# A two-layer hybrid encoder on one core: gate rows by block and head, and the first layer's row sums from a token-major copy of x

## The chip, the core and the metric

One Trainium2 chip, one of its cores. The metric is the device time of one execution of the program in microseconds, as the median of several runs.

## The reference, cut to what matters

512 tokens of width 1024 go through two layers. A layer normalises the rows of x, projects them to 6,928 columns, gives those to four mixers (A a gated linear recurrence, B windowed attention, C an mLSTM, D attention to 256 memory tokens), multiplies each by a SiLU gate, projects their concatenation back and adds x. The change touches two pieces.

```python
def _rmsnorm(x, g):
    xf = x.astype(F32)
    y = xf * lax.rsqrt(jnp.mean(xf * xf, axis=-1, keepdims=True) + EPS)
    return (y * g.astype(F32)).astype(x.dtype)
...
        b = jnp.cumsum(fb, axis=-1)
        d_intra = jnp.where(mask, b[..., :, None] - b[..., None, :] + ib[..., None, :], -jnp.inf)
        d_inter = b + m[..., None]
        m_t = jnp.maximum(jnp.max(d_intra, axis=-1), d_inter)
        w = jnp.einsum('bhtd,bhsd->bhts', qb, kb) * jnp.exp(d_intra - m_t[..., None])
        g = jnp.exp(d_inter - m_t)
```

The first is the row norm of layer 0. The second is C's gates: for 4 heads and 2 directions, running sums `b` of the log forget gates over 512 tokens and a running maximum `m_t` that stabilises the exponentials.

## The kernel before, in words

Everything works on float32 split into two float32r halves, hi and lo. A projection is three matmuls per 128-row step (hi by hi, hi by lo, lo by hi); `proj_ch` (L435) makes channel-major results 128x512, `proj_tok` (L399) token-major ones 128x256. `load_w` (L374) brings a weight block of 512 KB into a tile `wr` (3 buffers), ScalarE casts it to `wh`, VectorE subtracts to `wl` (3 buffers each).

The order of the work is made by a planner, `Weave` (L153): the main line emits projections and calls `tick` with their TensorE nanoseconds; jobs are generators that yield (TensorE time spent, latency until their next step), and a job's next step is emitted when the planned time has passed. The constants `G_LAT*`, `R_LAT*`, `M_LAT*` are those latencies. Each engine then runs its own queue in that order.

**The opening** (`start`, L1401). For each of 8 steps k: x^T's rows (`xs`, 128x512) and a weight step of 256 columns are loaded on SP's queue; ScalarE makes hi, VectorE lo of both; TensorE multiplies the *unnormalised* rows for the first A projection (six matmuls a step, tiles `o`). Beside it the squares of x^T go alternately to ScalarE and GpSimd, GpSimd and VectorE add them (`plus`, L1422), and `add_squares` (L470) sums over channels with four ones products (tile `tr`, 128x1). `rms4` and `diag` make 1/rms as a diagonal matrix and `spread` (L493) broadcasts it with one ones product to R, 128x512. All that is the job "R" (`rest`, L1458); after the spread it also forms the normalised rows `h` (`norm_k`, L504: a product with R on VectorE or, for odd k, GpSimd; hi on ScalarE; lo on VectorE), then the squares and the spread of the memory rows (Rm). Meanwhile the main line (`group_A`, L674; `gates`, L697) projects the two gate directions from the unnormalised rows and scales the results by R. The first projection on normalised rows is `values` (L713).

**C's gate chain** (`gate_chain`, L925), a job in each layer, woven among the window attention of B (`mix_B`, L788) and projections. Its rows are 4 heads at partitions 0 to 3 (forward) and 32 to 35 (backward), 512 tokens each: a polynomial for log(1+y), four transposes per 128 tokens (L950), four scans of 4x512 on VectorE, differences and exponentials, eight transposes back (L1013). The rows R and G go through HBM (`rdr`, `gdr`) to be broadcast later, the block decays through `ddr` to `dec`.

## Time and profile before

| | us |
|---|---|
| median of 3 runs | 1123.88 (1120.58 to 1124.38) |
| the profiled execution | 1126.58 |
| its span, first to last instruction | 1124.7 |
| TensorE busy | 1083.0 (96%) |
| VectorE busy | 780.0 (69%) |
| ScalarE busy | 538.7 (48%) |
| GpSimd busy | 140.8 (13%) |

The profile is of one execution. PE is TensorE's matmuls, PEld its weight loads, DVE VectorE, ACT ScalarE, POOL GpSimd, SP the queue that issues transfers. Matmuls are pipelined: one shows the time from start to end, and the next starts earlier. A bracket at the end of a timeline row is the idle time before it on its engine and what ended it. L142 is the line of a helper that records every operation of four engines, so rows are read by their tiles: `u` and `a` are work tiles, `pj`, `tr`, `s` and `o` the four kinds of PSUM tiles.

### The profile page before, as it was taken

Reading aid. Unit: us, or ns where it says so; the run is one execution under the profiler, and the core shown is the slowest. Engines: PE = TensorE matmul, PEld = TensorE weight load, DVE = VectorE, ACT = ScalarE, POOL = GpSimd, SP = SyncE. Lnnn points to the kernel's source line nnn. Section 1 sums busy time; section 2 is a strip of 40 time slices with the busy share of each in tenths; the row PEclk is TensorE's granted clock in tenths of the full one; section 3 lists DMA queues with packets and bytes.
Section 4 is the critical chain, followed back from the end, with each engine's and each line's share of the span. In section 5 each row is a group of like instructions: output and inputs, shape, how many; then the busy total and the mean of one; then the engine's idle time right before and its main releaser. Section 6 shows DMA issues by size and latency. Waiting matters only on the chain.

```text
span 1124.7 us, 22824 instructions
## 1 busy us (share of the span) xinstructions
PE 1083.0 (96%) x9142; PEld 972.2 (86%) x9142; DVE 780.0 (69%) x1815; ACT 538.7 (48%) x1138; POOL 140.8 (13%) x212
## 2 busy tenths in 40 slices
PE   6899999989999999999999999999899999999997
PEld 4699988989888797888788999889889788989997
DVE  7788546787476968777373676477858678687664
ACT  5544346656444444334554433376655353433443
POOL 4200000231000213011020000012200012120200
PEclk9899999999999999999999999999999999999999
DMA  7232134111221435222434221221122233362111
GB/s 260 76 114 77 57 112 133 59 58 58 94 66 56 120 105 170 92 90 87 138 129 134 76 79 56 94 78 57 40 75 78 76 90 108 94 197 86 66 38 75
DMA packets 34785, 105.44 MB, mean 94 GB/s; under 512 B 4360, under 2 KB 7816, under 8 KB 34680
## 3 DMA queue, kind: packets, MB, share of 16 engines
q1 hardware_dynamic: 33960, 101.57, 28.6%
q0 software_dynamic: 720, 2.42, 0.5%
q8 instruction: 72, 1.18, 0.4%
q14 instruction: 33, 0.27, 0.1%
HBM read 99.72 MB, written 4.26 MB: 92 GB/s over the span
## 4 chain that ended last, share of the span: by engine, by line
PE 77%; DVE 13%; ACT 3%; issue 2%; DMA 1%; POOL 0%; SPq 0%; DVEq 0%; ACTq 0%; POOLq 0%
PE pj L248 32%; PE pj L251 29%; DVE a L142 5%; PE o L248 4%; PE s L248 3%; PE s L251 3%; DVE u L142 3%; DVE wl L142 3%; PE tr L858 1%; PE o L251 1%; ACT a L142 1%; ACT wh L142 1%; ACT u L142 1%; DVE rq_t L142 1%; PE tr L1291 1%
## 5 line engine op out<-in xcount | busy, mean ns | idle before, releaser
L251 PE MATMUL pj<-wh,u 128*128 128x256 f32 x1984 | 389.2, 287 | 1.8 <-ACT u L142 1.2
L248 PE MATMUL pj<-u,wh 128*128 128x512 f32 (+1 forms) x1216 | 378.4, 392 | 1.2 <-ACT a L142 1.0
L251 PEld LDWEIGHTS pj<-wh,u 128*128 128x128 f32 x1984 | 316.7, 189 | 6.0 <-ACT u L142 1.6
L142 DVE TENSOR_TENSOR wl<-wr,wh 128x1024 fp32r<-128x1024 f32 (+1 forms) x162 | 197.0, 1217 | 132.0 <-ACT wh L142 130.9
L251 PE MATMUL pj<-wl,u 128*128 128x256 f32 x992 | 280.7, 283 | 0.0
L248 PEld LDWEIGHTS pj<-u,wh 128*128 128x128 f32 x1216 | 219.7, 191 | 43.0 <-ACT a L142 1.4
L142 ACT CAST wh<-wr 128x1024 fp32r<-128x1024 f32 (+1 forms) x162 | 164.2, 1014 | 154.4 <-PE pj L248 85.0
L248 PE MATMUL pj<-u,wl 128*128 128x512 f32 (+1 forms) x608 | 234.3, 385 | 1.8 <-DVE wl L142 1.8
L251 PEld LDWEIGHTS pj<-wl,u 128*128 128x128 f32 x992 | 188.3, 190 | 0.8 <-issue 0.3
L248 PEld LDWEIGHTS pj<-u,wl 128*128 128x128 f32 x608 | 115.4, 190 | 25.2 <-DVE wl L142 2.0
L142 DVE TENSOR_TENSOR u<-u,a 128x512 f32<-128x512 f32 (+1 forms) x104 | 74.1, 730 | 19.7 <-PE s L251 15.9
L142 POOL TENSOR_SCALAR u<-u,rB 128x256 f32<-128x256 f32 (+1 forms) x64 | 37.4, 597 | 240.6 <-DVE rB L142 137.2
L248 PE MATMUL pj<-wh,u 128*128 128x256 f32 (+1 forms) x320 | 62.8, 287 | 0.0
L248 PE MATMUL o<-u,u 128*128 128x129 f32 (+1 forms) x384 | 51.9, 281 | 2.1 <-DVE dnC L142 2.1
L248 PEld LDWEIGHTS o<-u,u 128*128 128x128 f32 x384 | 49.7, 196 | 4.7 <-issue 2.7
L142 POOL TENSOR_TENSOR u<-u,cf 128x512 f32<-128x512 f32 x16 | 24.2, 1510 | 234.1 <-DMA u<-rdr 234.1
L248 PEld LDWEIGHTS pj<-wh,u 128*128 128x128 f32 x320 | 51.0, 188 | 0.7 <-issue 0.5
L248 PE MATMUL pj<-wl,u 128*128 128x256 f32 (+1 forms) x160 | 45.3, 284 | 0.0
L142 DVE TENSOR_TENSOR u<-u,u 128x512 f32<-128x512 f32 (+2 forms) x48 | 38.8, 841 | 3.8 <-ACT a L142 2.6
L248 PE MATMUL s<-u,a 128*128 128x256 f32 (+1 forms) x224 | 41.3, 303 | 0.0
L251 PEld LDWEIGHTS s<-u,u 128*32 128x32 f32 (+1 forms) x1760 | 27.4, 115 | 14.9 <-issue 6.0
L142 DVE TENSOR_TENSOR u<-pj,u 128x256 f32<-128x256 f32 (+2 forms) x52 | 24.9, 502 | 21.4 <-PE pj L248 14.6
(212 smaller groups left out, 1440.2 us busy)
## 6 DMA issues: line engine op xcount, KB each, us to landing
wr<-in_wpk SPq DMA_DIRECT2D x154, 512.0 KB, 3.5
u<-in_xT SPq DMA_DIRECT2D x16, 256.0 KB, 4.5
u<-rdr SPq DMA_DIRECT2D x16, 256.0 KB, 4.6
u<-gdr SPq DMA_DIRECT2D x16, 192.0 KB, 4.5
u<-in_memT SPq DMA_DIRECT2D x4, 512.0 KB
xd<-u POOLq DMA_DIRECT2D x4, 512.0 KB, 5.2
u<-xd SPq DMA_DIRECT2D x4, 512.0 KB, 9.2
out<-u SPq DMA_DIRECT2D x8, 256.0 KB, 2.0
```

Of the source, the lines that this page charges most:

```text
L142: r = f(*args, **kw)
L248: nc.tensor.matmul(out, l, r, start=start, stop=stop)
L251: nc.tensor.matmul(out, l, r, start=start, stop=stop, skip_group_check=True)
L858: nc.tensor.transpose(pt[:, j * P:(j + 1) * P], pr[e][:, j * P:(j + 1) * P], ident)
L1291: nc.tensor.transpose(pt[:, (2 * t + i) * P:(2 * t + i + 1) * P], pr[:, i, t * P:(t + 1) * P], ident)
```

## The change

It has two parts.

C's gate chain keeps a row per block of 128 tokens and head: 16 rows at partitions 0 to 15 (forward), 16 at 32 to 47 (backward), each 128 tokens long. One transpose takes the place of four, the scans run over 128 tokens in 16 rows, and the carry from block to block is made by two matmuls of 48x49 (with constant matrices that say which block comes earlier), a masked add and a maximum. Two transposes bring the rows back. These tiles use the PSUM kind `o` in place of `tr`. G's exponential takes the carried maximum as its bias. The decays go to HBM and come back in 4-byte pieces, in another layout.

In the opening, x itself is loaded too, token-major, four tiles of 128x1024 (`xt`); ScalarE squares each with an accumulating output, which gives the row sums. The squares of x^T, their additions and the four ones products go. The normalised rows are a job of their own, "N", eight steps with 1.1 us planned between them, all products on VectorE; `gates` joins it before the mixers start. The squares of the memory rows follow the spread of R, and their spread becomes the first step of the job `mem_norm`.

```diff
-G_LAT0, G_LAT1, G_LAT2, G_LAT3, G_LAT4 = 2800, 1800, 2250, 2250, 3400
+G_LAT0, G_LAT1, G_LAT2, G_LAT3, G_LAT4 = 2800, 6500, 2500, 4500, 4500
...
-R_LAT0, R_LAT = 6000, 3500
-M_LAT, M_LAT2 = 20000, 2500
+R_LAT0, R_LAT = 0, 9000
+H_LAT = 1100
+M_LAT, M_LAT2 = 20000, 1500
...
             if pr == 0:
                 gates()
+                wv.join(*jobN)
+                jobN.clear()
...
-                for c in range(NC):
-                    nc.tensor.transpose(pt[0:100, c * P:(c + 1) * P], GP[:, c], ident)
-                act.copy(LI[0:36], pt[0:36])
-                act.copy(L[0:36], pt[64:100])
-                yield 0, G_LAT2
+                pt = po()
+                nc.tensor.transpose(pt[0:112, 0:P], GP, ident)
+                act.copy(LI[0:48], pt[0:48, 0:P])
+                act.copy(L[0:48], pt[64:112, 0:P])
+                yield 107, G_LAT2
...
-                dve.tensor_tensor_scan(M[0:4], L[0:4], LI[0:4], 0.0, ALU.add, ALU.max)
-                dve.tensor_tensor_scan(rev(M), rev(L), rev(LI), 0.0, ALU.add, ALU.max)
-                dve.tensor_tensor_scan(B[0:4], KM[0:4], L[0:4], 0.0, ALU.mult, ALU.add)
-                dve.tensor_tensor_scan(rev(B), rev(KM), rev(L), 0.0, ALU.mult, ALU.add)
+                dve.tensor_tensor_scan(B[0:16], one, L[0:16], 0.0, ALU.mult, ALU.add)
+                dve.tensor_tensor_scan(rev(B), ones[32:48], rev(L), 0.0, ALU.mult, ALU.add)
+                dve.tensor_tensor_scan(M[0:16], L[0:16], LI[0:16], NEG, ALU.add, ALU.max)
+                dve.tensor_tensor_scan(rev(M), rev(L), rev(LI), NEG, ALU.add, ALU.max)
+                ends = [(slice(32 * d, 32 * d + 16), (P - 1) * (1 - d)) for d in range(2)]
+                for r, e in ends:
+                    dve.tensor_scalar(X2[r, 0:49], succ[r], B[r, e:e + 1], None, ALU.mult)
+                    dve.tensor_scalar(X2[r, 49:98], ident[r, 0:49], M[r, e:e + 1], None, ALU.mult)
                 yield 0, G_LAT3
...
-                dve.tensor_tensor(R[0:36], B[0:36], M[0:36], ALU.subtract)
+                pS = po()[0:48, 0:49]
+                mm(pS, pred, X2[0:48, 0:49], start=True, stop=False)
+                mm(pS, ones[0:48, 0:48], X2[0:48, 49:98], start=False, stop=True)
...
+                dve.tensor_tensor(ca[0:48], pS, gmask, ALU.add)
+                dve.tensor_reduce(mb[0:48], ca[0:48], AX.X, ALU.max)
+                dve.scalar_tensor_tensor(M[0:48], B[0:48], mb[0:48], M[0:48], ALU.add, ALU.max)
...
+                dve.tensor_tensor(R[0:48], B[0:48], M[0:48], ALU.subtract)
...
-                for tt, n in ((TA, 100), (TB, 36)):
-                    pt = ptr()
-                    for c in range(NC):
-                        nc.tensor.transpose(pt[:, c * n:c * n + n], tt[0:n, c * P:(c + 1) * P], ident[0:n, 0:n])
...
+                yield 250, G_LAT4
+                pt = po()
+                nc.tensor.transpose(pt[:, 0:112], TA[0:112], ident[0:112, 0:112])
+                nc.tensor.transpose(pt[:, 112:160], TB[0:48], ident[0:48, 0:48])
...
         def mem_norm():
             yield 0, 0
+            spread(jobM.pop(0), Rm)
+            yield 450, M_LAT2
             mem0.append(mem_kv(0))
...
-                sqs.append(a2([512]))
-                if k % 2 == 1:
-                    act.activation(sqs[k], x, AF.Square)
-                    if k < 6:
-                        plus(gp, k - 1, k)
-                else:
-                    gp.tensor_tensor(sqs[k], x, x, ALU.mult)
-                if k == 5:
-                    plus(dve, 0, 2)
-                elif k == 7:
-                    for j in (4, 6, 7):
-                        plus(dve, 0, j)
...
+            xt, mt = [[u4([D]) for _ in range(n)] for n in (NC, 2)]
...
+            def squares(ts, ss):
+                for c, t in enumerate(ts):
+                    act.activation(t, t, AF.Square, accum_out=ss[:, c:c + 1])
...
             def rest():
 
+                squares(xt, sst)
                 with tc.high_priority():
-                    add_squares(sums, sqs[0], NC, True, True)
-                    dg = diag(rms4(sums[:, 0:NC]), NC)
-                yield 900, R_LAT
+                    dg = diag(rms4(sst), NC)
+                yield 0, R_LAT
                 with tc.high_priority():
                     spread(dg, R)
                     for b in range(2):
                         dve.tensor_tensor(q[b], pts[b], R, ALU.mult)
+                squares(mt, ssm)
+                jobM.append(diag(rms4(ssm, 2), 2))
+                jobN.append(wv.spawn("N", norms()))
+                yield 900, 0
+
+            def norms():
                 for k in range(8):
-                    norm_k(xs[k // 2][:, k % 2], k, R, 0, h, gp if k % 2 else dve)
+                    norm_k(xs[k // 2][:, k % 2], k, R, 0, h, dve)
+                    yield 0, H_LAT
```

The order moves in three places. First SP's queue in the opening; `wr_265`, `wr_271` (before) and `wr_250`, `wr_256` (after) are the weights of the first gate projection, `wr_403`, `wr_409` and `wr_361`, `wr_367` those of the second. Before:

```order
L142 DMA wr_265<-in_wpk 128x1024
L142 DMA wr_271<-in_wpk 128x1024
L142 DMA u_40_245<-in_mem 128x1024
L142 DMA u_41_246<-in_mem 128x1024
L142 DMA u_44_251<-in_cu 128x288
L142 DMA wr_403<-in_wpk 128x1024
L142 DMA wr_409<-in_wpk 128x1024
L142 DMA wr_473<-in_wpk 128x1024
```

After:

```order
L152 DMA wr_250<-in_wpk 128x1024
L152 DMA wr_256<-in_wpk 128x1024
L152 DMA u_30_220<-in_x 128x1024
L152 DMA u_31_221<-in_x 128x1024
L152 DMA u_32_222<-in_x 128x1024
L152 DMA u_33_223<-in_x 128x1024
L152 DMA u_34_224<-in_mem 128x1024
L152 DMA u_35_225<-in_mem 128x1024
L152 DMA u_40_236<-in_cu 128x288
L152 DMA wr_361<-in_wpk 128x1024
L152 DMA wr_367<-in_wpk 128x1024
L152 DMA wr_455<-in_wpk 128x1024
```

The four rows of x stand between the first projection's weights and everything that follows, and the second projection's weights are seven places behind.

Second, TensorE in the opening, inside the first gate projection (tiles `s_277`, `s_278` before, `s_262`, `s_263` after), which starts right after the 48 matmuls of the weight loop. Before, from behind its second matmul on:

```order
L251 MATMUL tr_137<-ones,a_31_145 128x1 x4
L248 MATMUL s_277<-u_5_98,wl_267 128x512
L248 MATMUL s_277<-u_5_98,wh_266 128x512
L248 MATMUL s_277<-u_9_102,wh_266 128x512
L248 MATMUL s_277<-u_5_98,wl_267 128x512
L248 MATMUL s_277<-u_6_99,wh_266 128x512
L248 MATMUL s_277<-u_10_103,wh_266 128x512
L248 MATMUL s_277<-u_6_99,wl_267 128x512
L248 MATMUL s_277<-u_6_99,wh_266 128x512
L248 MATMUL s_277<-u_10_103,wh_266 128x512
L248 MATMUL tr_330<-a_60_322,ones 128x512
```

After, from its twelfth matmul on:

```order
L258 MATMUL s_262<-u_6_99,wl_252 128x512
L258 MATMUL s_263<-u_5_98,wh_251 128x512
L258 MATMUL s_263<-u_9_102,wh_251 128x512
L258 MATMUL s_263<-u_5_98,wl_252 128x512
L258 MATMUL s_263<-u_5_98,wh_251 128x512
L258 MATMUL s_263<-u_9_102,wh_251 128x512
L258 MATMUL s_263<-u_5_98,wl_252 128x512
L258 MATMUL s_263<-u_6_99,wh_251 128x512
L258 MATMUL tr_315<-a_56_280,ones 128x512
L258 MATMUL s_263<-u_10_103,wh_251 128x512
```

The ones products (`tr_137`) are gone, and the spread of R (`tr_330`, now `tr_315`) stands behind 19 matmuls of this projection, where it was behind 11.

Third, VectorE at the gate chain of layer 0, from its first scan on. Scans print as SCALAR_TENSOR_TENSOR on tiles `a` with 4x512 (before) or 16x128 (after); `u<-tr` are attention's copies of its transposed weights. Before:

```order
L142 TENSOR_TENSOR seB_2945<-nmB_2933,par 128x2
L142 SCALAR_TENSOR_TENSOR a_458_2959<-a_448_2911,a_447_2910 4x512
L142 TENSOR_TENSOR wl_3142<-wr_3140,wh_3141 128x4x256
L142 SCALAR_TENSOR_TENSOR a_458_2959<-a_448_2911,a_447_2910 4x512
L142 TENSOR_TENSOR dnB_2942<-dnB_2942,seB_2945 128x2
L142 SCALAR_TENSOR_TENSOR a_459_2960<-a_460_2963,a_448_2911 4x512
L142 RECIPROCAL rB_2949<-dnB_2942 128x2
L142 SCALAR_TENSOR_TENSOR a_459_2960<-a_460_2963,a_448_2911 4x512
L142 TENSOR_TENSOR u_437_2841<-tr_2977,u_435_2839 128x3x128
L142 TENSOR_TENSOR u_438_2842<-tr_2983,u_436_2840 128x3x128
L142 TENSOR_TENSOR a_449_2912<-a_459_2960,a_458_2959 36x512
L142 TENSOR_TENSOR a_463_3001<-a_447_2910,a_459_2960 36x512
```

After:

```order
L152 SCALAR_TENSOR_TENSOR a_455_2960<-ones,a_453_2958 16x128
L152 TENSOR_TENSOR seB_2992<-nmB_2980,par 128x2
L152 SCALAR_TENSOR_TENSOR a_455_2960<-ones,a_453_2958 16x128
L152 SCALAR_TENSOR_TENSOR a_454_2959<-a_453_2958,a_452_2957 16x128 x2
L152 TENSOR_SCALAR a_458_2963<-cf,a_455_2960 16x49
L152 TENSOR_SCALAR a_458_2963<-cf,a_454_2959 16x49
L152 TENSOR_TENSOR dnB_2989<-dnB_2989,seB_2992 128x2
L152 TENSOR_SCALAR a_458_2963<-cf,a_455_2960 16x49
L152 RECIPROCAL rB_2996<-dnB_2989 128x2
L152 TENSOR_TENSOR u_469_3015<-tr_3017,u_467_3013 128x3x128
L152 TENSOR_SCALAR a_458_2963<-cf,a_454_2959 16x49
L152 TENSOR_TENSOR a_456_2961<-a_452_2957,a_455_2960 48x128
```

Before, a split of a weight block (`wl_`) and three more scans stand between the first scan and the two copies, and the 512-column differences behind them. Now four scans of 128 columns and three scalings of 49 columns stand ahead of a copy, and the split is no longer among them.

## Rows read from the trace of the kernel before

**Rows 1.** The page's busy times, and TensorE's busy tenths in 40 equal slices
```profile
PE 1083.0 (96%) x9142; PEld 972.2 (86%) x9142; DVE 780.0 (69%) x1815; ACT 538.7 (48%) x1138; POOL 140.8 (13%) x212
...
PE   6899999989999999999999999999899999999997
```

**Rows 2.** The page's chain that ended last, share of the span by engine
```profile
PE 77%; DVE 13%; ACT 3%; issue 2%; DMA 1%; POOL 0%; SPq 0%; DVEq 0%; ACTq 0%; POOLq 0%
```

**Rows 3.** Windows: stretch, us, busy (xinstructions) by engine, granted TensorE clock, DMA share, GB/s
```profile
6.00:14.00 8.00, 6.80 (x16) 5.07 (x17) 7.67 (x15) 7.61 (x16) 5.28 (x4) 1.00 1.02 368
...
26.00:31.00 5.00, 5.00 (x16) 3.55 (x16) 2.77 (x11) 1.38 (x3) 0.00 (x0) 0.66 0.34 111
...
31.00:44.00 13.00, 12.83 (x56) 10.04 (x54) 12.28 (x14) 7.92 (x11) 6.42 (x4) 1.00 0.23 78
...
44.00:51.00 7.00, 4.21 (x12) 3.36 (x13) 4.06 (x7) 3.48 (x5) 0.00 (x0) 0.76 0.25 75
...
50.00:75.00 25.00, 24.07 (x373) 22.27 (x372) 17.67 (x24) 13.77 (x22) 0.00 (x0) 0.98 0.33 107
...
70.00:100.00 30.00, 29.06 (x459) 27.29 (x459) 29.16 (x92) 16.89 (x26) 0.00 (x0) 1.00 0.23 75
...
250.00:255.00 5.00, 5.00 (x35) 5.00 (x34) 4.78 (x12) 1.62 (x3) 0.82 (x2) 0.75 0.02 7
```

**Rows 4.** Timeline of the opening: start us, us, engine, operation, xcount, [idle before <-releaser]
```profile
8.85 1.51 DVE L142 TENSOR_TENSOR wl<-wr,wh 128x256 fp32r<-128x256 f32 x1
...
13.63 0.39 PE L248 MATMUL o<-u,wl 128*128 128x512 f32 x1
...
17.49 0.41 DVE L142 TENSOR_TENSOR wl<-wr,wh 128x256 fp32r<-128x256 f32 x1
...
17.62 0.50 PE L248 MATMUL o<-u,wh 128*128 128x512 f32 x1 [1.23 <-DVE u L142]
...
18.17 1.06 ACT L142 ACTIVATE u<-u 128x1024 f32<-128x1024 f32 x1
...
18.49 0.68 DVE L142 TENSOR_TENSOR a<-a,a 128x512 f32<-128x512 f32 x1
...
25.39 1.02 PE L251 MATMUL tr<-ones,a 128*128 128x1 f32 x8 [1.72 <-DVE a L142]
...
29.49 1.57 PE L248 MATMUL tr<-a,ones 128*128 128x512 f32 x2
...
32.92 5.80 DVE L142 TENSOR_TENSOR a<-u,a 128x512 f32<-128x512 f32 x4
...
46.78 0.67 PE L248 MATMUL tr<-a,ones 128*128 128x256 f32 x2 [2.96 <-DVE a L142]
...
55.81 0.28 PE L251 MATMUL pj<-wh,u 128*128 128x256 f32 x1
```

**Rows 5.** Timeline of VectorE at layer 0's gate chain (first of four scans)
```profile
242.55 1.21 DVE L142 TENSOR_TENSOR_SCAN a<-a,a 4x512 f32<-4x512 f32 x1
...
248.76 1.02 DVE L142 TENSOR_TENSOR u<-tr,u 128x384 fp32r<-128x384 f32 x2
...
249.70 3.70 DVE L142 TENSOR_TENSOR a<-a,a 36x512 f32<-36x512 f32 x6
```

**Rows 6.** Timeline of TensorE at the gate chains of layers 0 and 1
```profile
240.23 0.62 PE L950 MATMUL tr<-cf,a 128*100 128x128 f32 x4 [0.78 <-DVE a L142]
...
249.46 0.88 PE L858 MATMUL tr<-cf,u 128*128 128x128 f32 x3 [2.60 <-DVE u L142]
...
789.99 0.61 PE L950 MATMUL tr<-cf,a 128*100 128x128 f32 x4 [1.18 <-DVE a L142]
...
799.22 0.88 PE L858 MATMUL tr<-cf,u 128*128 128x128 f32 x3 [2.60 <-DVE u L142]
```

**Rows 7.** The chain that ended last, in order of time, layer 0's last gate transposes
```profile
256.30 0.34 PE tr L1013 x4
...
258.92 0.38 PE tr L1013 x4
```

More of the change, by code (lines that the diff above doesn't have):

```diff
@@ L119, in const_arrays @@
     invf = np.broadcast_to(inv[None, :], (P, 8)).astype(np.float32)
-    cf = np.concatenate([ident, ge, np.zeros((P, P), np.float32), le, invf], axis=1)
+    r = np.arange(48)
+    d, c, hd = r // 32, r % 32 // 4, r % 4
+    ok = r % 32 < 16
+    early = (ok[:, None] & ok[None, :] & (d[:, None] == d[None, :]) & (hd[:, None] == hd[None, :])
+             & ((c[:, None] < c[None, :]) ^ (d[:, None] == 1)) & (c[:, None] != c[None, :]))
+    one = ok[:, None].astype(np.float32)
+    gm = np.zeros((P, 146), np.float32)
+    gm[0:48] = np.concatenate([early, early.T, one, np.where(early.T, 0.0, NEG), 0 * one], axis=1)
+    cf = np.concatenate([ident, ge, np.zeros((P, P), np.float32), le, invf, gm], axis=1)
     i, j = p % 32, q[:, :32]
@@ L468, in rms @@
             return r
-        def add_squares(ps, sq, n, first, last):
-            for c in range(n):
-                gmm(ps[:, c:c + 1], sq[:, c * P:(c + 1) * P], ones[:, 0:1], first and c == 0, last)
         def rms4(ss, n=NC):
@@ new lines, in gate_chain @@
+                X2 = a2([98])
+                for t in (M, B, X2, TA, TB):
+                    gp.memset(t, 0.0)
+                pt = po()
[3 more added lines that the diff above has]
+                yield 107, G_LAT2
+                def rev(t):
+                    s = t[32:48]
+                    return bass.AP(s.tensor, s.offset + P - 1, [list(s.ap[0]), [-1, P]])
+                one = ones[0:16]
@@ new lines, in gate_chain @@
+                for r, e in ends:
+                    act.activation(TB[r], TA[r], AF.Exp, bias=R[r, e:e + 1])
+                last_exp[:] = [act.activation(TA[64:112], M[0:48], AF.Exp, scale=-1.0)]
+                yield 250, G_LAT4
+                pt = po()
+                nc.tensor.transpose(pt[:, 0:112], TA[0:112], ident[0:112, 0:112])
+                nc.tensor.transpose(pt[:, 112:160], TB[0:48], ident[0:48, 0:48])
+                tm = a2([160])
+                act.copy(tm, pt[:, 0:160])
```

110 lines of the change are left out of this document (36 added, 74 removed).

## Prediction

> **What bounds the kernel now.** I read the busy times first: TensorE has something to run for 96% of the span [rows 1], so at most the last few per cent can be won by shorter waits, and the slices say where: TensorE's digits are low in the first two slices, in the last one, and dip in two places in the middle, one in each layer. The chain that ended last agrees: 77% of it is TensorE, 13% VectorE [rows 2]. An edit counts only if it removes TensorE time or a wait of TensorE.
>
> Next the windows [rows 3], which add what the slices hide: after each longer wait the granted clock drops. It is 0.66 in 26 to 31 us and 0.76 in 44 to 51 us, and 0.75 in the five microseconds after the mid-layer wait; the lower of the two levels is 1.2 GHz, the upper 2.4. At the upper level 56 matmuls of the opening projections take 12.83 us, 0.229 us each.
>
> Then the timeline of the opening [rows 4]. Read TensorE's rows down to 55.81 us, where the first matmul on normalised rows (`pj<-wh,u`) starts. Waits on VectorE precede the ones column sums (1.72 us), the fifth weight step (1.23 us) and the spread for the memory rows (2.96 us). VectorE is slow there: the 128x256 split takes 1.51 us at 8.85 us, while GpSimd squares rows of x, and 0.41 us at 17.49 us, when GpSimd is idle.
>
> Last the gate chain. On VectorE [rows 5] four scans of 4x512 at 1.21 us stand ahead of the two copies that attention's values wait for, then six operations of 3.70 us. On TensorE [rows 6] that is a wait of 2.60 us in both layers, and 0.78 and 1.18 us before the gate transposes.
>
> **The opening, step by step.** Removed: four squares and three sums on GpSimd, four squares on ScalarE, four sums on VectorE (0.68 us each), the four ones products on TensorE. VectorE then needs 0.41 us and one 128x512 operation (0.68 us the nearest row) per weight step, about 1.1 us, less than what TensorE needs at either level: six matmuls at 0.229 us are 1.4 us. So TensorE never waits in that loop. It reaches the upper level at 13.6 us, as before (the matmul of 13.63 us is the first of 0.39 us [rows 4]); 14 of the loop's 48 matmuls have started by then, and 34 at 0.232 us (0.229 and a little) take 7.9 us: the loop ends at 21.5 us.
>
> Added: four rows of x, 512 KB each, on SP's queue ahead of mem and of the weights of the second gate projection. The queues moved 368 GB/s in 6 to 14 us [rows 3]. At that rate from 3 us on, 3.9 MB of earlier data (eight weight steps of 384 KB, a block of 512 KB, constants) end at 13.5 us, the next block at 14.9, then x at 1.4 us a row, the last at 20.5. ScalarE squares each in 1.06 us (the row for mem [rows 4]), about 1.2 with the accumulator, and keeps pace: done at 21.7. From the end of the ones products to the spread it took 3.1 us before (26.41 to 29.49 us [rows 4]), with memory's chain mixed in; so the spread's operand stands at 24.8 us at the latest. TensorE reaches the spread in its order after 19 matmuls of the second projection, at 21.5 + 4.4 = 25.9 us: no wait, with 1.1 us to spare. The weights behind x: mem ends near 23.3, the two blocks at 25.1 and 26.5. Their casts stand on ScalarE behind the squares of mem and the copy of the spread (27.4 us); at 1.06 us for 1,024 columns they end at 28.5 and 29.6, and the splits on VectorE, 1.2 us each, by 31.5. TensorE needs the first at 33.6. The cover is 2 to 4 us.
>
> Two projections of 48 matmuls at 0.232 us are 22.3 us; the spread of R, 1.57 us at the low level, about 0.9 at the upper, and the one for the memory half of that: 21.5 + 22.3 + 1.3 = 45.1 us, against 55.8 now: **10.7 us**.
>
> What is late next is VectorE. All eight norm products go to it: eight at 0.68 are 5.4 us, where four beside GpSimd took 5.80 us [rows 4], so its total is as before. But when the projection on normalised rows starts, VectorE still owes three norm halves, three scalings and a split, 6 x 0.7 + 1.2 = 5.4 us, that were done by 55.8 us before; and in 70 to 100 us VectorE is busy 29.16 of 30 us [rows 3]. Against that it idled 7.3 us between 50 and 75 us (17.67 of 25 busy [rows 3]), and the scaling of the memory rows now stands behind the first levels of the mixers in its order. I take 1.5 us of new waits there; the bounds are 0 and the whole lag, 5 us. Opening: 10.7 - 1.5 = **9.2 us**.
>
> On the x rows one thing stays open. The trace shows a queue that moves 368 GB/s for eight microseconds; it doesn't show whether a transfer issued early also ends early. If each takes its turn, x is complete before the weights behind it, as in my sum. If transfers under way share the engines evenly, x's last row ends with the weights, at about 26.5 us: rival 2. The Trainium skill, DMA: Bandwidth & Descriptors, Queues, rings and completion order, says that each DMA engine consumes descriptors in ring order, though completion is not in order of issue; by the first half the sum stands, by the second alone it would be rival 2's.
>
> **The gate chain, per layer.** Twelve transposes (0.62, 0.34 and 0.38 us of the chain [rows 6, 7]) become three, and two small products are added; a transpose of such a group costs about 0.11 us, a product of 49 columns in full precision at most two of them, so 1.3 - 0.33 - 0.4 = 0.6 us less. The scans have 128 columns in place of 512. From 0.41 us for 256 columns and 0.68 for 512 an operation is some 0.15 us and 1.04 ns a column; the scan's 1.21 us then falls to 0.15 + 1.06 / 4 = 0.42, with bounds 0.15 and 1.21. The six later operations become about nine of 0.28 us (bounds 0.15 and 0.62). VectorE: 8.5 us before, 4.2 after, and in the new order the two copies stand ahead of and between them, so the 2.60 us go. With them go (1 - 0.75) x 5 = 1.25 us of low clock [rows 3], and the 0.98 us (mean) before the gate transposes, which now stand about 20 rows later. In return TensorE waits in order for two new hops, the product with the block ends and the last transposes. No row shows them. Between the product and the transposes the order has 26 projection matmuls of half length (0.12 us), ten transposes and four scores, some 4.8 us, and I count 5 to 6 us of queued steps on VectorE and ScalarE; bounds 0 and 4.6 us, the old stretch from the copies to the end of the six operations (248.76 to 253.40 us [rows 5]). I take 1.4, near the difference of the two counts with one more step queued. Sum 2.60 + 1.25 + 0.98 + 0.6 - 1.4 = **4.0 us**, in two layers 8.1.
>
> At nothing: the wider constant load, GpSimd's smaller memsets, and the transfers of the gate rows and decays (their readers run 100 us later). The decay copy in 4-byte pieces would count only if it held up the weight block behind it by more than that block's lead.
>
> **Sum.** 9.2 + 8.1 = 17.3 us. The profiled execution took 1126.58 us, 1124.7 of it span, so 1109.3; it lay 2.7 us above the median of 1123.88, which makes **1106.6 us**.
>
> **The rivals.**
> 1. *The waits only move to the new hops.* If each hop makes TensorE wait like the old scans, 3 us more a layer: 1106.6 + 6 = 1112.6. For it: the hops stand in TensorE's order, and VectorE's queue there stays full. Against: VectorE's work halves.
> 2. *x is late.* The last row at 26.5 us puts the spread's operand at 26.5 + 1.2 + 3.1 = 30.8 and TensorE's wait at 4.9 us, with some 1.25 us of low clock behind it: 1106.6 + 6.2 = 1112.8. For it: nine large transfers in a row on one queue. Against: the queue holds its rate for eight microseconds of such rows.
> 3. *VectorE becomes the bound in the first mixers*, with the full lag: 3.5 us more, 1110.1.
> 4. *Slower.* The chain through the two hops decides. The gates lose when the wait per layer exceeds 5.4 us, and the whole is slower by over 0.5% when it exceeds 5.4 + (9.2 + 5.6) / 2 = 12.8 us; at 14 us it is 9.2 + 2 x (5.4 - 14) = -8.0, or 1131.9. For it: ten small steps, each behind another on two queues. Against: the old chain, with scans three times as long, took 16 us from its first transposes to its last, and the new order leaves some 15 us of matmuls there.
> 5. *Nothing to measure*: several of 1 to 3 together, 1119 to 1125.
>
> **How the numbers follow.** Chances: forecast 0.62, rival 1 0.12, rival 2 0.10, rival 3 0.05, rival 4 0.05, rival 5 0.06. A difference of 0.5%, 5.6 us, is about what a measurement can tell from none, so faster means below 1118.3. Forecast and rivals 1 to 3 lie there, 0.89, less 0.03 for their upper tails: faster 0.86, same 0.09, slower 0.05. The range: with no new wait at all the gain is 10.7 + 2 x 5.4 = 21.5, which is 1102.4, and some other short waits of TensorE may go too: 1100. At the other end rivals 1 and 2 alone give about 1113, and one of them with half of the other 1116: 1117. Outside lie rivals 4, 5 and some tails, under 0.2.
>
> **What would show it.** Right: the first `pj<-wh,u` on normalised rows near 45 us; granted clock near 1 from 20 to 50 us; the split at 0.41 us throughout; scans near 0.4 us; no wait of over 1 us in TensorE's rows near 235 and 785 us. Wrong: a wait before the spread of R or before the second gate projection (rival 2); waits on VectorE between 55 and 90 us (rival 3); waits before the 48x49 product or the last gate transposes (rivals 1 and 4). The forecast falls if the first matmul on normalised rows comes after 50 us, or if TensorE's idle time in either mid-layer stretch stays above 3 us.

## The result, and the profile after

The changed kernel took **1106.24 us** (median of 4 runs, 1104.43 to 1108.0) where the kernel before took 1124.13 us in the same comparison (4 runs): a ratio of 0.9843, 95% interval 0.9811 to 0.9875. A second comparison gave 0.9838 (0.9814 to 0.9862). The forecast was 1106.6 us, in a range of 1100 to 1117. The profiled execution took 1105.7 us, 1103.8 of it span; that of before took 1126.58, so the two traces differ by 20.9 us, 3 us more than the medians do.

The page of the changed kernel: busy times, TensorE's busy tenths and its granted clock in 40 slices, and the chain that ended last by engine.

```profile
PE 1070.9 (97%) x9124; PEld 961.8 (87%) x9124; DVE 761.7 (69%) x1821; ACT 540.5 (49%) x1144; POOL 116.0 (11%) x189
...
PE   7999999999999999999989999999999999999997
...
PEclk9999999999999999999999999999999999999998
...
PE 76%; DVE 13%; ACT 4%; DMA 4%; issue 2%; SPq 0%; POOL 0%; ACTq 0%; DVEq 0%; POOLq 0%
```

Against [rows 1] and [rows 2] the digits of the first two slices and those of the two mid-layer stretches rose (one near 565 us fell from 9 to 8); TensorE is still three quarters of the chain. Where the time came from is read by setting the same matmul of the program (the n-th of a kind) of both traces side by side. The lead of the changed kernel is 9.5 us at the first product on normalised rows, 11.1 us near 90 us of before, 7.2 us from 150 us to the gate stage of the first layer, 12.0 us behind it, 13.6 us ahead of the second layer's gate stage and 18.9 us behind that. So in these two traces **the opening kept 7.2 us, the gate stages gave 4.7 and 5.3 us**, and the rest, some 3.5 us, lies in stretches that the change doesn't touch; the profiled execution of before also lay 2.5 us above its median.

The opening, timeline of the changed kernel (start us, us, engine, operation, xcount, [idle before <-releaser]): ScalarE's four squares of x, the spread of the sums, the spread for the memory rows, and the first product on normalised rows.

```profile
12.48 0.42 DVE L152 TENSOR_TENSOR wl<-wr,wh 128x256 fp32r<-128x256 f32 x1
...
19.08 1.06 ACT L152 ACTIVATE u<-u 128x1024 f32<-128x1024 f32 x1
...
20.36 1.06 ACT L152 ACTIVATE u<-u 128x1024 f32<-128x1024 f32 x1
...
21.64 1.06 ACT L152 ACTIVATE u<-u 128x1024 f32<-128x1024 f32 x1
...
22.92 1.06 ACT L152 ACTIVATE u<-u 128x1024 f32<-128x1024 f32 x1
...
26.08 1.10 PE L258 MATMUL tr<-a,ones 128*128 128x512 f32 x2 [0.34 <-DVE a L152]
...
45.17 0.70 PE L258 MATMUL tr<-a,ones 128*128 128x256 f32 x2
46.30 0.36 PE L261 MATMUL pj<-wh,u 128*128 128x256 f32 x1 [0.43 <-ACT Rm L152]
```

Where before had waits of 1.23, 1.72 and 2.96 us [rows 4], 0.34 and 0.43 us are left, and the split stays at 0.42 or 0.43 us. The windows of the changed kernel (stretch, us, busy by engine, granted clock, DMA share, GB/s) show a granted clock of 1.00 up to 75 us, where before had 0.66 and 0.76 [rows 3], and one new dip, in 75 to 100 us:

```profile
0.00:10.00 10.00, 2.61 (x5) 1.78 (x6) 3.22 (x13) 4.76 (x9) 2.36 (x9) 1.00 0.79 254
10.00:20.00 10.00, 10.00 (x40) 7.99 (x39) 7.88 (x13) 7.75 (x13) 0.00 (x0) 1.00 1.00 384
20.00:30.00 10.00, 9.65 (x40) 7.24 (x39) 4.27 (x14) 8.93 (x18) 0.00 (x0) 1.00 0.77 312
30.00:50.00 20.00, 19.57 (x100) 15.99 (x100) 19.78 (x30) 14.88 (x23) 0.00 (x0) 1.00 0.39 118
50.00:75.00 25.00, 25.00 (x507) 23.75 (x509) 21.33 (x46) 11.29 (x19) 0.00 (x0) 1.00 0.28 89
75.00:100.00 25.00, 23.15 (x357) 21.97 (x348) 20.93 (x60) 11.84 (x19) 0.90 (x1) 0.93 0.27 94
```

The dip is one wait. VectorE stood 1.80 us for the load of the memory rows, with a mixer's step behind it in its order, and TensorE stood 1.85 us for that step (timeline):

```profile
77.34 0.48 DVE L152 SCALAR_TENSOR_TENSOR u<-u,pg,Rm 128x256 f32<-128x256 f32 x1 [1.80 <-DMA u<-in_memT]
...
84.05 0.56 PE L261 MATMUL s<-u,u 128*32 128x32 f32 x32 [1.85 <-DVE rr L152]
```

The gate stage. First the windows of before, first layer and then second:

```profile
225.00:240.00 15.00, 14.33 (x115) 13.89 (x113) 12.47 (x43) 9.40 (x23) 4.39 (x8) 1.00 0.23 72
240.00:250.00 10.00, 7.17 (x58) 7.03 (x58) 9.74 (x19) 5.80 (x13) 5.15 (x10) 0.95 0.16 54
250.00:260.00 10.00, 10.00 (x78) 9.80 (x77) 7.55 (x20) 5.65 (x14) 1.76 (x4) 0.88 0.11 26
260.00:275.00 15.00, 14.75 (x121) 14.14 (x120) 11.92 (x37) 11.29 (x32) 2.96 (x6) 1.00 0.16 57
772.00:790.00 18.00, 16.45 (x133) 16.04 (x131) 14.01 (x48) 10.31 (x27) 5.16 (x10) 1.00 0.19 60
790.00:800.00 10.00, 7.40 (x58) 7.23 (x59) 9.77 (x18) 5.80 (x13) 5.11 (x10) 0.93 0.16 54
800.00:812.00 12.00, 12.00 (x96) 11.80 (x96) 9.36 (x28) 7.95 (x22) 1.76 (x4) 0.92 0.16 47
812.00:826.00 14.00, 13.64 (x105) 12.47 (x104) 11.18 (x32) 9.78 (x26) 2.96 (x6) 1.00 0.12 39
```

The windows of the changed kernel, from and to the same matmuls of the program:

```profile
217.77:232.00 14.23, 14.02 (x115) 13.85 (x114) 11.72 (x39) 9.40 (x23) 4.16 (x9) 1.00 0.21 75
232.00:247.00 15.00, 15.00 (x128) 14.69 (x127) 14.02 (x44) 10.64 (x27) 2.69 (x7) 1.00 0.10 38
247.00:263.02 16.02, 15.10 (x123) 14.40 (x122) 11.46 (x39) 11.52 (x32) 2.98 (x8) 1.00 0.24 68
758.39:775.00 16.61, 16.42 (x133) 16.25 (x132) 12.91 (x43) 10.31 (x27) 5.04 (x10) 1.00 0.19 65
775.00:790.00 15.00, 15.00 (x128) 14.66 (x127) 14.02 (x47) 10.72 (x28) 2.68 (x7) 1.00 0.11 36
790.00:807.10 17.10, 16.13 (x125) 14.89 (x124) 12.50 (x38) 12.24 (x34) 2.98 (x8) 1.00 0.22 65
```

In the first layer 50.0 us became 45.25. TensorE's idle time fell from 3.75 us (50 less 46.25 busy) to 1.13, and the low clock, 0.05 and 0.12 of ten microseconds or 1.7 us, is gone. In the second layer 54.0 us became 48.7, idle 4.51 to 1.16, and 0.07 x 10 + 0.08 x 12 = 1.7 us of low clock is gone. That this low clock belongs to the old gate chain is not shown; experiment 1 has the same waits without it. The chain itself, on VectorE and TensorE (timeline, first layer): scans of 0.43 and 0.41 us for 1.21 us [rows 5], the product with no wait, and 0.83 us in front of the last transpose.

```profile
239.13 0.43 DVE L152 TENSOR_TENSOR_SCAN a<-ones,a 16x128 f32<-16x128 f32 x1
...
240.08 0.86 DVE L152 TENSOR_TENSOR_SCAN a<-a,a 16x128 f32<-16x128 f32 x2
...
244.43 0.29 PE L258 MATMUL o<-a,cf 48*48 48x49 f32 x2
...
249.93 0.26 PE L1014 MATMUL o<-cf,a 112*128 112x112 f32 x1
...
251.39 0.26 PE L1015 MATMUL o<-cf,a 48*128 48x48 f32 x1 [0.83 <-ACT a L152]
```

### The profile page after: what moved, and what is told of

Its sections match the earlier page's. It is cut to its first block, busy times and chain, and to the rows that moved or that the text cites. A ratio compares the mean times of both kernels' runs of the same rounds, so it can differ in the third digit from the quotient of the medians.

```text
span 1103.8 us, 22774 instructions
## 1 busy us (share of the span) xinstructions
PE 1070.9 (97%) x9124; PEld 961.8 (87%) x9124; DVE 761.7 (69%) x1821; ACT 540.5 (49%) x1144; POOL 116.0 (11%) x189
## 3 DMA queue, kind: packets, MB, share of 16 engines
q8 instruction: 72, 1.18, 0.4%
## 4 chain that ended last, share of the span: by engine, by line
PE 76%; DVE 13%; ACT 4%; DMA 4%; issue 2%; SPq 0%; POOL 0%; ACTq 0%; DVEq 0%; POOLq 0%
PE pj L258 31%; PE pj L261 28%; PE s L258 4%; DVE u L152 4%; PE o L258 4%; DVE a L152 4%; DVE wl L152 3%; PE s L261 3%; PE o L261 2%; PE tr L866 1%; ACT u L152 1%; ACT wh L152 1%; ACT a L152 1%; DMA u<-in_memT 1%; DMA u<-in_x 1%
## 5 line engine op out<-in xcount | busy, mean ns | idle before, releaser
L152 DVE TENSOR_TENSOR wl<-wr,wh 128x1024 fp32r<-128x1024 f32 (+1 forms) x162 | 193.9, 1198 | 126.0 <-ACT wh L152 124.8
L258 PEld LDWEIGHTS pj<-u,wh 128*128 128x128 f32 x1216 | 216.9, 188 | 43.6 <-ACT u L152 2.6
```

Of the source, the lines that this page charges most:

```text
L152: r = f(*args, **kw)
L258: nc.tensor.matmul(out, l, r, start=start, stop=stop)
```

## The experiments

Ratios are to the kernel before, run on the same chip beside them, with 95% intervals. 0.001 is 1.1 us.

**1. Each half alone.** The first kernel is the changed one with the gate chain of before (its constants, latencies and readers too), the second is the kernel of before with the new gate chain. The lines show each against the changed kernel, cut to the latencies.

```diff
 # opening only
-G_LAT0, G_LAT1, G_LAT2, G_LAT3, G_LAT4 = 2800, 6500, 2500, 4500, 4500
+G_LAT0, G_LAT1, G_LAT2, G_LAT3, G_LAT4 = 2800, 1800, 2250, 2250, 3400
...
 # gates only
-R_LAT0, R_LAT = 0, 9000
-H_LAT = 1100
-M_LAT, M_LAT2 = 20000, 1500
+R_LAT0, R_LAT = 6000, 3500
+M_LAT, M_LAT2 = 20000, 2500
...
```

> Only the opening is changed (sums from the token-major copy of x, norm rows as a job); the gate chain, its constants and its latencies are as before. From the two traces, the lead over the kernel before at the same matmul of the program is 9.5 us at the first product on normalised rows, 11.4 us near 90 us of before, and 8.1 us from 105 us to the gate stage. Theory: the opening is worth these 8.1 us whatever the gate chain is, so about 1124.1 - 8.1 = 1116 us, ratio 0.9928; TensorE's wait of 1.85 us near 84 us is there again, and in the middle of each layer the old waits of 2.6 us stand. The prediction's own term was 9.2 us (1114.9). Rival: the lead is taken back at the old gate waits, because weight blocks or VectorE work come no earlier there: 1120 us or more.

> Only the gate chain is changed (rows by block and head, its constants, latencies and readers); the opening is as before. The two traces put 4.9 us on it in the first layer (lead 8.1 us before, 13.0 us after the stage) and 6.0 us in the second (14.2 to 20.2 us): about 1124.1 - 10.9 = 1113 us, ratio 0.9903. The prediction's own terms gave 8.1 us (1116). With the opening alone the two must then make 18 to 19 us if they don't touch each other. Rival: part of the gain in the gate stage comes only with the new opening (another phase of weight loads): less than 8 us here.

Measured: the opening alone 1115.36 us, 0.9926 (0.9902 to 0.995), 8.3 us; the gates alone 1117.17 us, 0.9933 (0.9909 to 0.9957), 7.5 us. Together 15.8 us, against 17.7 and 18.2 us for the changed kernel: within the intervals the halves add. The leads from which both expectations start are about 1 us too high after 105 us; matched matmul by matmul they are the 7.2, 12.0, 13.6 and 18.9 us above. The gates' 7.5 us (4.8 to 10.2) is below the 10.9 expected and in the band of the rival, less than 8 us; but their trace gives 4.8 and 5.3 us in the two stages, as with the new opening, so that rival is not needed. The 10.9 was read against a profiled execution of before that lay 2.5 us above its median.

In the opening's trace the first product on normalised rows starts at 45.44 us, where the prediction had 45.1. The old waits in the middle of the layers are there as expected, but the granted clock behind them is 1.00, not 0.88 and 0.92 (timeline, then windows):

```profile
238.79 0.52 PE L856 MATMUL tr<-cf,u 128*128 128x128 f32 x3 [2.60 <-DVE u L143]
...
787.84 0.52 PE L856 MATMUL tr<-cf,u 128*128 128x128 f32 x3 [2.62 <-DVE u L143]
```

```profile
239.00:249.00 10.00, 9.99 (x86) 9.61 (x85) 8.48 (x23) 6.38 (x17) 1.78 (x5) 1.00 0.18 55
...
788.00:800.00 12.00, 11.89 (x100) 11.34 (x100) 10.44 (x31) 8.29 (x24) 1.83 (x5) 1.00 0.17 48
```

These two stages are 0.9 and 1.0 us shorter than in the trace of before with the same gate chain. So of the 4.7 and 5.3 us some 3.9 and 4.3 are left against this trace: the low clock is something that one execution had and another had not.

The wait near 84 us that I expected there again was only 0.41 us, though VectorE's order at it is the same, which opened the question of experiment 2.

**2. The wait near 84 us.** Two attempts at its cause. The first makes the job that normalises the memory rows due 3 us later; the second issues its two loads where the first mixers are queued, four weight blocks earlier on SP's queue.

```diff
 # due later
-M_LAT, M_LAT2 = 20000, 1500
+M_LAT, M_LAT2 = 23000, 1500
 # loaded earlier
-                    jobM.append(wv.spawn("memn", mem_norm(), after=M_LAT))
+                    jobM.append(wv.spawn("memn", mem_norm(mem_load()), after=M_LAT))
...
+        def mem_load():
             mts = [u4([4, 256]) for _ in range(2)]
             for i in range(2):
+                sy.dma_start(mts[i], a["memT"][:, 4 * i:4 * i + 4])
+            return mts
```

> The changed kernel with the job that normalises the memory rows due 3 us later (20,000 to 23,000). In the changed kernel VectorE stood 1.80 us at 75.5 us for the load of the memory rows, with a mixer's step behind it in its order; TensorE then waited 1.85 us at 84 us and its clock was 0.83 over the ten microseconds around it. Theory: that queue position is the cause of the 3.1 us which the opening's lead loses there; with the mixer's step ahead of seven of the eight scalings the wait at 84 us falls under 0.5 us and the time by 2 to 3.5 us, to 1103 to 1104 us. Rival: VectorE is short of time in the first mixers as such (it was busy 28 of 30 us there), so the wait only moves to the next step: within 1 us of the changed kernel.

> The changed kernel with the two loads of the memory rows issued when the first mixers are queued, four weight blocks earlier on SP's queue, and nothing else written differently. In the run with the memory job due later VectorE still waited 2.0 us for these loads and TensorE 1.53 us behind it, so that run didn't test the cause; the position of the load on SP's queue does. Theory: the loads land late because they stand behind weight blocks whose buffers come free late (issued at 70.8 us, needed at 75.5 us, there at 77.3 us); issued some 15 us earlier they are there, VectorE doesn't wait for them, TensorE's wait near 84 us falls under 0.5 us, the granted clock of 75 to 100 us is 1.00, and the time falls by 2 to 3.5 us, to 1103 to 1104 us. Rival: VectorE has too much to do in the first mixers, and the wait comes back at the next mixer's step: within 1 us. A second risk: the weight blocks behind the moved loads come later, which would show as TensorE waiting for a split of weights between 55 and 80 us.

> The changed kernel itself, unedited, to stand beside the next two on the same chip: 1106 us, ratio 0.984 to 0.985. TensorE's wait near 84 us depends on when the memory rows land: in the five profiles so far of kernels with this order VectorE waited 0.36, 1.0, 1.2, 1.6, 1.8 and 3.1 us for them there (the first with the opening alone), so it should again lie between 0.4 and 3.2 us.

> The kernel with the memory rows loaded earlier, a second time, beside the changed kernel on one chip, since the first comparison put it 1.7 us ahead with intervals that overlap. Theory: its first products of the mixers no longer depend on a transfer that lands by chance, so it is 1.5 to 3 us faster (1103 to 1104.5 us), without TensorE's wait near 84 us. Rival: the gain of 3.1 us at that place is lost again further on, where its lead over the changed kernel shrank to 0.8 us between 620 and 940 us of the trace: under 1 us.

Due later: 1105.55 us, 0.9832 (0.9808 to 0.9855), and no test of the cause, since one scaling kept its place: VectorE still waited 2.01 us for the load and TensorE 1.53 us at the step behind. Loaded earlier: 1104.45 us, 0.9828 (0.9804 to 0.9852), and the second time 1105.23 us, 0.9832 (0.9813 to 0.9852), beside 1104.72 us, 0.9838 (0.9814 to 0.9862), of the changed kernel itself.

The cause of the wait is shown. Across executions with one order at this place TensorE's wait follows VectorE's wait for the load, 0.04 or 0.05 us longer each time: 0.36 and 0.41, 0.93 and 0.98, 0.98 and 1.03, 1.17 and 1.22, 1.62 and 1.67, 1.80 and 1.85, 2.04 and 2.08, 3.14 and 3.18 us. With the loads earlier it is gone in all three traces. The two ends of that list, the opening alone and the kernel of experiment 5 (timelines):

```profile
75.14 0.48 DVE L143 SCALAR_TENSOR_TENSOR u<-u,pg,Rm 128x256 f32<-128x256 f32 x1 [0.36 <-DMA u<-in_memT]
...
81.85 0.46 PE L252 MATMUL s<-u,u 128*32 128x32 f32 x32 [0.41 <-DVE rr L143]
```

```profile
77.61 0.48 DVE L152 SCALAR_TENSOR_TENSOR u<-u,pg,Rm 128x256 f32<-128x256 f32 x1 [3.14 <-DMA u<-in_memT]
...
84.31 0.46 PE L261 MATMUL s<-u,u 128*32 128x32 f32 x32 [3.18 <-DVE rr L152]
```

With the earlier load (issued at 42.2 us, for 70.8) the windows of the first of these traces have no idle time of TensorE and no low clock, and VectorE does the scalings in time that it had free:

```profile
50.00:75.00 25.00, 25.00 (x489) 23.78 (x487) 24.50 (x50) 13.07 (x21) 0.00 (x0) 1.00 0.24 79
75.00:100.00 25.00, 25.00 (x394) 23.58 (x394) 21.92 (x64) 11.62 (x21) 0.89 (x1) 1.00 0.26 85
```

The price is not what I expected: the two traces lead the first one of the changed kernel by 3.1 and 4.2 us at 150 us, and its second one by 0.4 and 1.5 us, but the ratios beside it differ by 0.0015 and 0.0006, 1.7 and 0.7 us, less than the intervals hold (the second time the medians even stand the other way, by 0.5 us). So the rival of the second expectation, under 1 us, can't be told from its theory; of the 3.1 us lead 2.2 are left at the end. The two traces of the changed kernel itself are 0.4 us apart at 50 us, 2.7 from 100 to 350 us and 0.8 to 2.0 after 375 us. A wait of 1 to 3 us is no larger than what executions of one kernel differ by.

**3. The distances in the gate chain.** The changed kernel with the old latencies: the same instructions, with the hops closer together in TensorE's order.

```diff
-G_LAT0, G_LAT1, G_LAT2, G_LAT3, G_LAT4 = 2800, 6500, 2500, 4500, 4500
+G_LAT0, G_LAT1, G_LAT2, G_LAT3, G_LAT4 = 2800, 1800, 2250, 2250, 3400
```

> The changed kernel with the old four latencies of the gate chain (1800, 2250, 2250, 3400 in place of 6500, 2500, 4500, 4500): same instructions, but on TensorE the gate transpose, the 48x49 product and the last transposes stand closer together, the product before the four 128x256 products of mixer and some 25 matmuls earlier. Theory of the prediction (rival 1's mechanism): the work itself is short, and the distance in order is what keeps the two hops from being waited for; with the old distances TensorE waits 1.5 to 3 us in front of the product or of the last transposes in each layer, and the time grows by 3 to 7 us against the changed kernel (1109 to 1113 us). Rival: the smaller steps alone did it (scans of 0.42 us for 1.21 us, three transposes for twelve), and the latencies are worth nothing: within 1.5 us of the changed kernel.

Measured: 1111.85 us, 0.989 (0.9866 to 0.9913), 5.3 us behind the changed kernel's 0.9843. TensorE's rows of the first layer (timeline) show the waits back, on the new instructions; the second layer's are 0.82, 1.63 and 0.45 us:

```profile
231.07 0.29 PE L958 MATMUL o<-cf,a 128*112 128x128 f32 x1 [0.79 <-DVE a L152]
...
239.44 0.26 PE L258 MATMUL o<-a,cf 48*48 48x49 f32 x2 [1.64 <-DVE a L152]
...
245.47 0.23 PE L1015 MATMUL o<-cf,a 48*128 48x48 f32 x1 [0.45 <-ACT a L152]
```

That is 2.9 us a layer for 0.83. In the trace the stages gave 2.6 and 2.9 us, where the changed kernel's gave 4.7 and 5.3. Rival 1 of the prediction describes this kernel; what keeps it away from the changed one is the distance. The rival named in the expectation, that the small steps alone did it, falls.

**4. The order inside the chain.** The keys' exponentials ahead of those of the decays; then this together with the earlier load.

```diff
+                dve.tensor_tensor(TA[0:48], LI[0:48], B[0:48], ALU.subtract)
+                for r, e in ends:
+                    act.activation(TB[r], TA[r], AF.Exp, bias=R[r, e:e + 1])
+                last_exp[:] = [act.activation(TA[64:112], M[0:48], AF.Exp, scale=-1.0)]
                 for d in range(2):
                     for src, dst in ((R, rdr), (G, gdr)):
```

> The changed kernel with the two exponentials of the keys' factors issued ahead of those of the decays and ahead of the transfers, in the gate chain. In the changed kernel TensorE waited 0.83 us in each layer in front of the second of the last two transposes, which reads these; ScalarE ran the decays' exponentials (0.81 us) just before. Theory: that order is the wait; it falls under 0.3 us in each layer, worth 1 to 1.6 us. Rival: the transpose, which also moves three matmuls up in TensorE's order, then waits for the exponentials all the same: less than 0.5 us.

> Memory rows loaded earlier and the keys' exponentials first in the gate chain, together. With the latter alone the wait in front of the last transposes fell from 0.83 to 0.31 and 0.34 us, and waits of 0.6 us of the mixer's transposes behind VectorE came up, with no gain in the time. Theory: the two are independent; the sum is that of the earlier load, 1103 to 1104.5 us, and at most 0.5 us better. Rival: the two waits of 0.5 us add to it: 1102 to 1103 us.

Measured: 1106.7 us, 0.9853 (0.9825 to 0.988), and together 1104.32 us, 0.9834 (0.9812 to 0.9856). The wait fell from 0.83 to 0.34 and 0.31 us, but waits in front of the mixer's transposes, 0.4 us in two in the changed kernel, came to 1.5 us in four with the new order alone. No gain in the time can be told: the first expectation's rival, less than 0.5 us, and the second's theory, at most 0.5 us better, stand.

**5. VectorE's time in the chain.** The four scans, each done three times: twelve of 0.42 us, 5.0 us, about the 4.8 us of the four old ones.

```diff
                 one = ones[0:16]
+                for _ in range(3):
-                dve.tensor_tensor_scan(B[0:16], one, L[0:16], 0.0, ALU.mult, ALU.add)
+                    dve.tensor_tensor_scan(B[0:16], one, L[0:16], 0.0, ALU.mult, ALU.add)
...
```

> The changed kernel with each of the four scans of a layer done three times: eight more scans of 0.42 us, 3.4 us of VectorE, between the gate copies and the 48x49 product; TensorE's order is the same. It puts back some of the VectorE time that the short scans removed. Theory of the prediction (VectorE's queue in the middle of the layer is what TensorE waits for): in the changed kernel the last operand of the product was ready at 242.6 us and the product ran at 244.4 us, 1.8 us of slack; 3.4 us more make TensorE wait about 1.6 us in front of the product or of the mixer's step behind it in each layer, 3 to 5 us in all with the lower clock after the waits (1109 to 1111 us). Rival: with the two copies for attention's values ahead of the scans the length of the scans no longer matters: under 1 us.

Measured: 1112.09 us, 0.9891 (0.9866 to 0.9916), 5.4 us more than the changed kernel, a little above what I expected. TensorE waited in the first layer (timeline)

```profile
244.82 0.26 PE L258 MATMUL o<-a,cf 48*48 48x49 f32 x2 [1.54 <-DVE a L152]
...
249.17 0.51 PE L258 MATMUL s<-u,a 128*128 128x256 f32 x2 [0.78 <-DVE nmB L152]
...
253.38 0.26 PE L1016 MATMUL o<-cf,a 48*128 48x48 f32 x1 [1.38 <-ACT a L152]
```

and the same within 0.05 us in the second: 3.7 us a layer for 0.83, or 5.7 us in all. Of the 3.4 us added per layer 1.5 were waited for at the product, as the slack of 1.8 us said; the later steps, which I had left out, pass the delay on. So the distances alone don't do it either: long scans eat part of them, and the rival, under 1 us, falls.

**6. Two costs that the prediction put at nothing.** The 146 new constant columns loaded apart from the first constants, behind the memory rows; and x loaded behind mem.

```diff
-        gp.dma_start(cf, a["cf"])
+        gp.dma_start(cf, a["cf"][:, 0:4 * P + 8])
...
+            sy.dma_start(gcon, a["cf"][0:48, 4 * P + 8:4 * P + 154])
 # the other kernel
-            for name, ts in (("x", xt), ("mem", mt)):
+            for name, ts in (("mem", mt), ("x", xt)):
```

> The changed kernel with the 146 new constant columns taken out of the constant load that starts the kernel and loaded by a transfer of their own (28 KB) behind the memory rows. In the runs with the wide load the first VectorE work waited for its parameters until 6.5 to 7.2 us (6.3 without it), the second weight step started at 8.18, 8.19, 8.23 and 8.84 us (7.96 and 7.99 without it), and the first product on normalised rows came at 46.3 us in the changed kernel against 45.44 us in the kernel with the opening alone. Theory: the wide load, which the prediction costed at nothing, costs 0.3 to 0.9 us in the opening; the second weight step starts at 8.0 us, the first product on normalised rows comes at 45.3 to 45.7 us and the time falls by 0.5 to 1 us (1105.2 to 1105.7). Rival: the differences in the first 10 us are scatter between executions, and the start doesn't move.

> The changed kernel with the four token-major rows of x loaded behind the two rows of mem instead of ahead of them, 1 MB later on the queue. The planner moves the spread of the sums 17 matmuls later in TensorE's order. It asks whether rows land in the order of issue, and what the opening's cover is worth. In order (theory of the prediction): the first square of x starts 2.5 us later (21.6 us for 19.08), the spread runs near 30 us for 26.08, the norm products end 3 to 4 us later, and VectorE's lag in the first mixers grows by that: 1 to 4 us slower (1107 to 1110). If transfers under way share the engines evenly (rival 2's rule), the squares start as before, and the time is within 1 us of the changed kernel. Third: in order, but the lag disappears in VectorE's idle time of the first 60 us, also within 1 us, with the squares 2.5 us later.

The narrow load: 1106.63 us, 0.9847 (0.9821 to 0.9872), no difference. The second weight step started at 8.09 us; the three kernels without the wide load lie at 7.96 to 8.09, the eleven with it at 8.17 to 8.84. So it may cost a tenth or a few there. But the first product on normalised rows came at 45.82 us, where kernels with the wide load had 45.18 to 46.60, so for the time the rival stands.

x behind mem: 1107.59 us, 0.9854 (0.9831 to 0.9876), 0.0016 above the changed kernel beside it, within the intervals. ScalarE's squares of the two rows of mem started at 17.68 and 18.96 us, those of x at 20.35, 21.51, 22.79 and 24.07, each within 0.15 us of its row's landing: one row after the other, in the order of issue. The first square of x came 1.3 us later, not 2.5, because the weight block ahead had landed 1.4 us earlier in that execution. The first product on normalised rows still started at 45.44 us. The cover held; the third case of the expectation fits.

No version ran faster than the changed kernel by more than the intervals leave open.

## Why the prediction was right, step by step

- *The loop ends at 21.5 us*: 21.15. The first matmul of 0.39 us came at 12.60 (13.63 forecast), but with 11 matmuls of the loop started and not 14. The split stayed at 0.42 or 0.43 us with GpSimd idle, and one wait of 0.67 us stood at the second weight step, where before had 0.59. This bears out what the prediction read from 1.51 and 0.41 us [rows 4]. The Trainium skill, SBUF — State Buffer, SBUF: two separate sides, says that a VectorE operation with two inputs in SBUF and a GpSimd operation that reads SBUF hold one pair of ports in turn, each for its whole instruction; the trace agrees, 1.51 us beside GpSimd's squares [rows 4] and 0.42 without them.
- *x's last row lands at 20.5 us, squared by 21.7*: **mis-sized**. The squares ran to 24.1 us. By the landing signals in the trace the rows landed at 19.06, 20.33, 21.61 and 22.90 us, and each square starts 0.02 to 0.03 us later. The rate was not at fault: 254 GB/s is 2.54 MB in the first 10 us, where 368 GB/s from 3 us on makes 2.58, and a row took 1.28 us, better than 1.4. The two gate blocks ahead were already late, landed at 16.56 and 17.80 us for 13.5 and 14.9. The step that failed takes a transfer as landed when the bytes up to it have moved at the mean rate. Each transfer's landing is sixteen signals in the trace, which for the last row came between 20.77 and 22.90 us, while bytes of the next transfer were moving; in the kernel with x behind mem the same spread was 1.2 us. Why it differs is open. The bytes were also summed 0.2 MB short, which is 0.5 us. The rows landed in the order of issue, as the forecast had it and rival 2 did not. The Trainium skill, DMA: Bandwidth & Descriptors, Queues, rings and completion order, says that each DMA engine consumes descriptors in ring order; the order of these landings agrees with it.
- *The spread's operand at 24.8 us, no wait, 1.1 us to spare*: a wait of 0.34 us. The steps behind the squares took 1.9 us (24.07 to 25.93), where 3.1 had been allowed, which by luck made up for half of the late row.
- *The second gate weights*: cast by 29.9 us (29.6 forecast), split by 32.4 (31.5), and not waited for at 33.76, where TensorE first read them.
- *The first product on normalised rows at 45.1 us*: 46.30, and 45.18 to 46.60 over the other executions. The two spreads with their waits took more than the 1.3 us allowed: the one for the memory rows, with two small matmuls beside it, 1.4 us, from the last matmul of the projection at 44.9 to 46.30, with 0.43 us of it a wait for the copy. That term, 10.7 us, came out at 9.5.
- *1.5 us of new waits in the first mixers, since VectorE is late*: **wrong in its reason**, and its size is that of one execution: the lead went from 9.5 to 7.2 us in the first trace of the changed kernel, and from 9.8 to 10.0 in the second. The sign that the prediction named for rival 3, a wait of TensorE for VectorE between 55 and 90 us, did show at 84 us. But VectorE had no lag that TensorE felt; it stood idle for the memory rows' load, and TensorE behind it. With the load earlier VectorE did the same work with no wait of TensorE. Rival 3 falls with that, at least up to 100 us.
- *The scans at 0.42 us*: 0.43 and 0.41. Between bounds of 0.15 and 1.21 the price by columns held.
- *The 2.60 us, the 0.98 us and the low clock go*: all three went. The clock's term is the weak one: against the profiled execution of before it is 1.7 us in each layer, since 1.25 us counted only five microseconds behind the wait; against the trace of experiment 1, with the same waits and a clock of 1.00 behind them, it is nothing. Without it the forecast's terms make 2.8 us a layer, and against that trace 3.9 and 4.3 were found: 3.0 and 3.5 of idle time and 0.9 and 0.8 of TensorE's work, which had been put at 0.6. The eleven runs of before beside that experiment went from 1120.23 us at a mean granted clock of 0.996 to 1128.12 at 0.986.
- *1.4 us at the new hops*: 0.83 and 0.82 us, none at the product. This term and the clock's, 0.57 and 0.45 us, with waits ahead of the gate transposes of 0.78 and 1.18 us for the mean of 0.98, are the difference between the 4.0 us forecast a layer and the 4.7 and 5.3 us found against the trace of before.
- *At nothing: the wider constant load*: borne out by experiment 6 as far as 1 us can be told. The small memsets and the gate transfers weren't tried alone.

In the sum the opening came 2.0 us short (7.2 for 9.2) and the gates 1.9 us over (10.0 for 8.1), in the traces; in the medians, halves alone, 8.3 (5.6 to 11.0) and 7.5 us against 9.2 and 8.1. The mechanisms of both halves are borne out and each term lies in its interval. That the total came within 0.4 us is luck: the terms are known to a microsecond or two, and errors of that size cancelled between the halves and inside each.

## What to carry to other kernels

A chain of small steps on one engine, read by another at fixed places in its order, has two handles, the length of the steps and the distance of the readers; here taking back either one cost some 5 us of what both gave. The low clock behind a wait is no fixed price: price the wait itself, count the clock over the whole stretch behind it, and look in a second trace whether it is there again. And before blaming a busy engine for a wait, read what it stood for: a load issued late behind other loads looks like an engine that is late, and moves from execution to execution.

## What the runs showed of the hardware that I had not expected

The landing of one transfer scatters. The first of the two loads of the memory rows (512 KB) was issued at 70.80 us and there at 77.3 in the changed kernel, 6.5 us later; with the opening alone it was issued at 69.91 and there at 75.1, 5.2 us later, and 1.6 MB moved in the ten microseconds around in both. The DMA view of the changed kernel, 69 to 79 us in 40 slices, shows a dip to 98 and 49 GB/s near 73 us with the rows under way:

```profile
GB/s 0 0 0 0 66 0 0 0 0 147 180 180 393 360 393 344 98 49 180 147 131 262 295 213 279 328 311 311 344 295 229 197 213 262 131 66 16 0 0 0
```

The same view with the opening alone, 68 to 78 us, has none once the rows move:

```profile
GB/s 0 0 0 0 0 66 0 0 0 49 180 66 213 360 393 410 377 344 328 311 344 213 213 213 229 361 410 410 377 311 148 33 0 66 0 0 0 0 49 147
```

What makes the dip is open; it wasn't tried.

The clock's fall behind a wait is not a matter of its length alone. Waits of 2.60 us were followed by 0.88 and 0.92 in the trace of before and by 1.00 in that of the opening alone. At the same place of the program a wait of 1.85 us was followed by a granted clock of 0.93 in 75 to 100 us and one of 2.08 us by 0.93, but the longest, 3.18 us in the kernel of experiment 5, by none (window of that kernel), and the 32 scores behind it took 0.46 us where they took 0.56 and 0.59 behind the other two:

```profile
75.00:100.00 25.00, 21.82 (x331) 20.70 (x330) 21.60 (x61) 11.31 (x18) 0.90 (x1) 1.00 0.27 91
```
